# The opening of a two-block forward pass: sums on TensorE, modulation chunks on VectorE, loads behind the weight tiles

## The chip, the cores and the metric

The kernel runs on one core of a Trainium2 chip, in one launch. The metric is the device time in microseconds. Each instruction is issued on one of five engines, each in its own order: TensorE (PE; its weight loads are shown as PEld), VectorE (DVE), ScalarE (ACT), GpSimd (POOL) and SyncE (SP), from whose queue all the loads are issued.

## The reference

Two blocks work on 256 tokens of width 2048 in fp32. The opening computes the keys and values of the memory for a cross-attention, which are needed much later, and what the first product of the first block needs: the modulation and the root mean square of x.

```
mkv   = rms_norm(mem, g_mem) @ w_mem_kv          # 256 x 2048 @ 2048 x 1024
c_act = silu(c)
mod   = c_act @ w_ada + b_ada                    # 2048 x 6144
shift, scale, gate = split(mod, 3)
h     = rms(x, norm_g) * (1 + scale) + shift
proj  = h @ w_in                                 # 2048 x 8192: the next phase
```

Then come attention, a gated recurrence, the output product, and a second block with a latent attention, the cross-attention and a feed-forward part.

## The kernel before, in words

Weights come in tiles of 1 MB (four chunks of 128 rows, 512 columns) into three buffers `wr`. A product in nearly full precision is made of three: each weight tile is split into hi, a cast by ScalarE (`wh`), and lo, the remainder, a subtraction by VectorE (`wl`); the activations have hi and lo too. `split_w` does this for half a tile, two chunks; `job` then issues its matmuls. In the opening (phase `mem`) such a half is 12 matmuls with 512 columns. There are three buffers of `wh` and two of `wl`, so the lo piece of a half waits until TensorE is through with the half before last.

The opening multiplies eight tiles of `w_mem_kv`, four for K and four for V in turn, by the memory (`mH`, `mL`, made in `load_mem` by `gsplit`, lines 316 and 317). Beside it stands `front()`, a generator which `linear` advances after each tile. It does three things by the table `FRONT`. First it loads eight tiles of `w_ada`, scale and shift in turn (`ada_steps((4, 0), ...)`), and adds their chunks, each times its column of `cact`, into an accumulator: the scale's all on VectorE (`V`), of the shift's tile one on VectorE and three as a product on ScalarE and an addition on GpSimd (lines 387 to 391). `ada_sum` adds the accumulators over the partitions by matmuls against a matrix of ones, and VectorE takes one column of each. Second it loads x. Third it finds the token sums: `sumsq` squares on ScalarE and adds four tiles into one on GpSimd (line 250), for x and likewise for the memory; `token_R` sums over the partitions by 8 matmuls with 128 columns of ones, GpSimd makes the inverse root (`inv_rms`), VectorE scales an identity by it, and a matmul spreads it as `R2`. At the end `make_h(0)` scales x by `gs` and `R2` and adds the shift.

The order on each engine is set by a scheduler from the order in which the code issues the instructions and from their dependences. SP's queue keeps its order too: a load whose buffer is not free holds all behind it.

Of the kernel before, what the change touches and what calls it, by code (L numbers as in the profile page):

```python
# [13 lines left out]
AF = mybir.ActivationFunctionType  # L14
# [3 lines left out]
P = 128  # L18
T = 256
# [13 lines left out]
AHEAD = dict(mem=0, pass0=0, pass3=1, gz=0, az=1, out=0, in2=1, mla=1, o=0, ffn=1, down=0)  # L33
BUDGET = dict(mem=0.3, pass0=0.5, pass3=2.0, gz=1.3, az=1.1, out=0.5, in2=0.1, mla=0.9, o=0.6, ffn=0.1, down=0.3)


GATES = ("VVVV", "VVVV", "VVVV", "VVVV")
PAIR = ("VVVV", "VVVV")

EARLY = 3  # L40
GSTART = 10
FRONT = (2, 0, 1, 0, 1, 1, 3, 2)

LAG = 5
COST = (0.5, 0.4, 1.0, 0.7, 1.3)
# [15 lines left out]
def trunk_kernel(ctx, tc, a, out):  # L61
# [64 lines left out]
        S.copy(hi, src)  # L126
        V.tensor_tensor(lo, src, hi.bitcast(F32), ALU.subtract)

    jobs = deque()

    def submit(job):

# [8 lines left out]
    def tile_mm(src, kc0, kt, cw, mode, banks, act, first, last, pre=None, post=None, mid=None):  # L141

        raw = load(src, kt, cw)
        n = 2 if mode == "N" else cw // P
        nk = 4 if cw == 256 else 2

        def one(kc, b, hi, lo):
            xh, xl, xx = act(kc0 + kc)  # L150
            hi, lo = hi[:, kc % nk, :], lo[:, kc % nk, :]
            st, sp = first and kc == 0, last and kc == kt - 1
            if mode == "T":
                o = banks[b // 2][:, (b % 2) * T : (b % 2) * T + T]
                s = slice(b * P, b * P + P)
                trip = ((o, hi[:, s], xh), (o, hi[:, s], xl), (o, lo[:, s], xh))
                st = st and b % 2 == 0
            elif mode == "T2":
                s = slice(b * P, b * P + P)
                trip = ((two(banks[b]), hi[:, s], xx), (banks[b][:, :T], lo[:, s], xh))  # L160
            else:
                o = banks[b][:, :cw]
                s = slice(b * P, b * P + P)
                trip = ((o, xh[:, s], hi), (o, xh[:, s], lo), (o, xl[:, s], hi))
            for i, (d, l, r) in enumerate(trip):
                PE.matmul(d, l, r, start=st and i == 0, stop=sp and i == len(trip) - 1, skip_group_check=True)  # L166

        def job(k, hi, lo):
            if k == 0 and pre is not None:
                pre()  # L170
            if not banks:
                banks.extend(bank("mm") for _ in range((cw // P + 1) // 2 if mode == "T" else 2))
            pairs = [(kc, b) for kc in range(k, k + nk) for b in range(n)]
            if last and k + nk == kt:
                pairs.sort(key=lambda p: p[1])
            for kc, b in pairs:
                one(kc, b, hi, lo)
            drain(BUDGET[phase[0]])
            if k + nk == kt and post is not None:
                post()  # L180
            elif mid is not None:
                mid()

        for k in range(0, kt, nk):
            hi, lo = split_w(raw, k, cw, mode)
            submit(lambda k=k, hi=hi, lo=lo: job(k, hi, lo))
# [34 lines left out]
    def token_R(work, R, rc):  # L221


        ps = bank("ax")
        for tb in range(2):
            for k in range(4):
                PE.matmul(ps[:, tb * P : tb * P + P], work[:, k, tb * P : tb * P + P], ones, start=k == 0, stop=k == 3,  # L227
                          skip_group_check=True)
        for tb in range(2):
            V.tensor_copy(rc[:, tb : tb + 1], ps[:, tb * P : tb * P + 1])  # L230
        inv_rms(rc, rc, 1.0 / D, EPS)
        if R is None:
            return
        dg = tmp([P, 2, P], "R")
        for tb in range(2):
            V.tensor_scalar(dg[:, tb, :], ident, rc[:, tb : tb + 1], None, ALU.mult)

        def spread():
            ps = bank("ax")[:, :T]
            PE.matmul(ps, ones, flat(dg), start=True, stop=True)  # L240
            S.copy(R, ps)
        return spread
# [67 lines left out]
    cact = hpool.tile([P, DC], F32, tag="cact", name="cact")  # L310
    rm = hpool.tile([P, 2], F32, tag="rm", name="rm")
    ssm = hpool.tile([P, 4, 2], F32, tag="ssm", name="ssm")
    sums = slot("s7", [P, 8, T])

    def gsplit(j, gname, x, H, L):
        S.activation(H, x, AF.Identity, scale=col(gname, j))
# [26 lines left out]
    def load_mem(kg):  # L343
        c = slice(4 * kg, 4 * kg + 4)
        SP.dma_start(mem[:, c, :], a["memT"][:, c, :])
        for k in range(4 * kg, 4 * kg + 4):
            gsplit(k, "g_mem", mem[:, k, :], mH(k), mL(k))
        sumsq(mem[:, c, :], kg, sums[:, 0:4, :], work[:, 8:12, :])


    def load_x(j):
        c = slice(4 * j, 4 * j + 4)
        x = xt[j // 2][:, 4 * (j % 2) : 4 * (j % 2) + 4, :]
        SP.dma_start(x, a["xT"][:, c, :])
        sumsq(x, j, sums[:, 4:8, :], work[:, 12:16, :])

    n_ada = [0]

# [9 lines left out]
            return ada_raw[n_ada[0] % 2]  # L368
        return None

    def ada_tile(ng, kg, accs, plan):

        raw = ada_buf(ng)
        if raw is None:
            raw = load(a["w_ada"][ng, kg], 4, 512)
        else:
            SP.dma_start(raw, a["w_ada"][ng, kg].rearrange("p (k c) -> p k c", k=4))
        def chunk(k):
            cc = cact[:, 4 * kg + k : 4 * kg + k + 1]
            first = kg == 0 and plan[k] not in plan[:k]  # L380
            if plan[k] == "V":
                if first:
                    V.tensor_scalar(accs[0], raw[:, k, :], cc, None, ALU.mult)
                else:
                    V.scalar_tensor_tensor(accs[0], raw[:, k, :], cc, accs[0], ALU.mult, ALU.add)  # L385
            elif first:
                S.mul(accs[1], raw[:, k, :], cc)
            else:
                t = tmp([P, 512], "pts")
                S.mul(t, raw[:, k, :], cc)  # L390
                G.tensor_tensor(accs[1], accs[1], t, ALU.add)

        for k in range(4):
            chunk(k)
            if k == 1:
                yield

    def ada_sum(ng, accs):
        ps = bank("ax")
        for j in range(4):  # L400
            for i, acc in enumerate(accs):
                PE.matmul(ps[:, j * P : j * P + P], acc[:, j * P : j * P + P], ones, start=i == 0, stop=i == len(accs) - 1,  # L402
                          skip_group_check=True)
        V.tensor_tensor(modT[:, 4 * ng : 4 * ng + 4], ps.rearrange("p (j n) -> p j n", j=4)[:, :, 0],
                        colr("b_ada", 4 * ng, 4), ALU.add)

    def ada_steps(ngs, plans):

        accs = []
        for i, plan in enumerate(plans):  # L410
            if ngs[0] >= 8:
                one = tmp([P, 512], "acc", 1)
                accs.append((one, gate_acc2(ngs[0])) if len(set(plan)) == 2 else (one, one))
                continue
            work = slot("s8", [P, 2, 512]) if i else None
            accs.append((tmp([P, 512], "acc", 1) if i == 0 else work[:, 0], work[:, 1] if i else tmp([P, 512], "acc", 1))
                        if len(set(plan)) == 2 else (tmp([P, 512], "acc", 1) if i == 0 else slot("s8", [P, 512]),) * 2)
        for kg in range(4):
            for i, ng in enumerate(ngs):
                yield from ada_tile(ng, kg, accs[i], plans[i])  # L420
                if kg == 3 and i:
                    yield
                    yield
                if kg == 3:
                    f = lambda ng=ng, i=i: ada_sum(ng, accs[i][: len(set(plans[i]))])
                    if ng < 8:
                        f()
                    else:
                        later(0.1, lambda f=f, ng=ng: (f(), done.add(f"g{ng}")), evq)
# [17 lines left out]
    acth = lambda kc: pair_of(h1[0], kc)  # L447

    def front():
        steps = ada_steps((4, 0), ("VVVV", "VPPP"))  # L450
        for i, n in enumerate(FRONT):
            for _ in range(2 * n):
                next(steps, None)
            if 1 <= i <= 4:
                load_x(i - 1)
            if i == 5:
                spread = token_R(sums[:, 4:8, :], R2, r2)
            if i == 6:
                spread()
            if i == 7:  # L460
                make_h(0)
            yield
            yield

    S.activation(cact, colr("c"), AF.Silu)
    linear([(lambda kg: a["w_mem_kv"][0, kg], 512, "N", ev_memk),
            (lambda kg: a["w_mem_kv"][1, kg], 512, "N", ev_memv)], range(4), lambda kc: (mH(kc), mL(kc), None),
           ahead=load_mem, aside=front(), done_loads=lambda: token_R(sums[:, 0:4, :], None, rm))


    lbt = hpool.tile([P, 3, 8], F32, tag="lbt", name="lbt")
# [335 lines left out]
    def gate_steps():  # L807
        for ng in range(8, 12):
            while ng == 11 and not xp:
                yield  # L810
            yield from ada_steps((ng,), (GATES[ng - 8],))
            while f"g{ng}" not in done:
                yield

# [3 lines left out]
    def modulate(kg, n):  # L818

        if len(steps) == kg:  # L820
            steps.append(ada_steps((4 + kg + 1, kg + 1), PAIR) if kg < 3 else gates)
        if n % 4 < EARLY and (kg < 3 or n >= GSTART):
            next(steps[-1], None)

# [636 lines left out]
```

## Time and profile before

| what | us |
|---|---|
| median of 3 runs | 1591.23 |
| lowest and highest of them | 1588.77, 1593.85 |
| the profiled execution | 1593.98 |
| its span in the trace | 1592.20 |
| busy in the span: TensorE | 1534.7 |
| busy: VectorE, ScalarE, GpSimd | 1165.7, 823.0, 280.5 |

A row of a timeline gives the start in the span, the time that the merged instructions took, engine, line, operation, the tile written and those read, and in brackets how long the engine had stood idle and what it had waited for. The matmuls of one row overlap, so a row lasts longer than the distance to the next one. In a row by stretch, PEclk is the mean granted clock: 1.00 is 2.4 GHz and 0.50 is 1.2.

### The profile page before, as it was taken

To read this page: it belongs to the slowest core of one execution; us is meant where nothing else is said; L and a number is where in the kernel's file an instruction comes from. 1 tells how busy PE (TensorE), PEld (TensorE's weight loads), DVE (VectorE), ACT (ScalarE), POOL (GpSimd) and SP (SyncE) were. 2 spreads that over 40 slices of the span, in tenths; PEclk is the share of its full clock that TensorE was granted. 3 is DMA by queue.
4 is the path that set the end of the run, shared out by engine and by line. 5 is a ranking of instruction groups with operands and counts; after the bars stand their busy time and mean duration, and the time that the engine had idled before them with its cause. 6 is when DMAs were issued, how large, how long until landed. Compare 5 with 4: busy or idle time off the path is not lost.

```text
span 1592.2 us, 24722 instructions
## 1 busy us (share of the span) xinstructions
PE 1534.7 (96%) x9730; PEld 1384.7 (87%) x9730; DVE 1165.7 (73%) x1671; ACT 823.0 (52%) x1194; POOL 280.5 (18%) x309
## 2 busy tenths in 40 slices
PE   5799999999899999999999999999999999999998
PEld 4588988978889999987999888888888888888887
DVE  7788999899997778568667667667667667445444
ACT  6365443664546745468545555555555555333332
POOL 3500000156532011413001111111111111000000
PEclk9899999999999999999999999999999999999999
DMA  9478888444555476444435555555555555556553
GB/s 386 197 271 334 330 303 330 169 152 169 222 197 211 174 266 236 174 160 143 150 134 184 185 192 205 186 190 203 189 189 204 190 188 200 196 186 214 207 185 133
DMA packets 50803, 331.67 MB, mean 208 GB/s; under 512 B 5632, under 2 KB 7936, under 8 KB 13312
## 3 DMA queue, kind: packets, MB, share of 16 engines
q1 hardware_dynamic: 50688, 330.10, 57.4%
q8 instruction: 76, 1.25, 0.3%
q14 instruction: 39, 0.32, 0.1%
HBM read 327.98 MB, written 2.10 MB: 207 GB/s over the span
## 4 chain that ended last, share of the span: by engine, by line
PE 85%; DVE 9%; issue 2%; POOL 2%; ACT 2%; DMA 1%; SPq 0%; DVEq 0%; ACTq 0%; POOLq 0%
PE mm L166 80%; DVE wl L122 3%; DVE acc L385 2%; DMA wr<-in_w_mem_kv_dram 1%; ACT wh L121 1%; PE ax L731 1%; DVE y L732 1%; PE ax L227 1%; PE ax L529 1%; PE ax L402 1%; DVE R L704 0%; DVE y L712 0%; PE ax L521 0%; PE ax L257 0%; DVE s L317 0%
## 5 line engine op out<-in xcount | busy, mean ns | idle before, releaser
L122 DVE TENSOR_TENSOR wl<-wr,wh 128x1024 fp32r<-128x1024 f32 (+2 forms) x516 | 652.5, 1266 | 321.9 <-PE mm L166 298.9
L121 ACT CAST wh<-wr 128x1024 fp32r<-128x1024 f32 (+2 forms) x516 | 534.6, 1040 | 495.4 <-PE mm L166 421.1
L166 PE MATMUL mm<-h,wh 128*128 128x512 f32 (+1 forms) x2560 | 687.3, 342 | 0.9 <-ACT wh L121 0.9
L166 PE MATMUL mm<-h,wl 128*128 128x256 f32 x1984 | 551.4, 278 | 10.9 <-DVE wl L122 10.9
L166 PEld LDWEIGHTS mm<-h,wh 128*128 128x128 f32 x2560 | 441.8, 189 | 56.6 <-ACT wh L121 1.5
L166 PEld LDWEIGHTS mm<-h,wl 128*128 128x128 f32 x1984 | 373.4, 188 | 13.5 <-DVE wl L122 13.4
L166 PE MATMUL mm<-f,wh 128*128 128x512 f32 x704 | 239.4, 389 | 0.0
L166 PE MATMUL mm<-wh,h 128*128 128x512 f32 (+1 forms) x704 | 218.8, 386 | 0.0
L166 PE MATMUL mm<-f,wl 128*128 128x256 f32 x704 | 194.3, 276 | 0.0
L166 PE MATMUL mm<-y,wh 128*128 128x256 f32 x1024 | 182.5, 282 | 0.6 <-ACT wh L121 0.6
L166 PEld LDWEIGHTS mm<-y,wh 128*128 128x128 f32 x1024 | 155.6, 189 | 0.9 <-ACT wh L121 0.8
L166 PEld LDWEIGHTS mm<-f,wh 128*128 128x128 f32 x704 | 132.2, 188 | 27.7
L166 PEld LDWEIGHTS mm<-wh,h 128*128 128x128 f32 x704 | 131.4, 188 | 24.5
L166 PE MATMUL mm<-y,wl 128*128 128x256 f32 x512 | 142.9, 280 | 2.6 <-DVE wl L122 2.5
L166 PE MATMUL mm<-wl,h 128*128 128x512 f32 (+1 forms) x352 | 135.6, 385 | 2.4 <-DVE wl L122 2.3
L166 PEld LDWEIGHTS mm<-f,wl 128*128 128x128 f32 x704 | 132.2, 188 | 0.0
L166 PEld LDWEIGHTS mm<-y,wl 128*128 128x128 f32 x512 | 96.5, 189 | 3.5 <-DVE wl L122 3.4
L1299 POOL TENSOR_TENSOR gp<-sg,R 128x256 f32<-128x256 f32 x44 | 36.1, 822 | 314.2 <-DVE sg L1298 314.2
L166 PEld LDWEIGHTS mm<-wl,h 128*128 128x128 f32 x352 | 66.3, 188 | 15.9 <-DVE wl L122 4.3
L166 PE MATMUL mm<-wh,s 128*128 128x512 f32 x128 | 45.3, 434 | 9.8 <-ACT wh L121 9.8
L385 DVE SCALAR_TENSOR_TENSOR acc<-wr,cact,acc 128x512 f32<-128x512 f32 x60 | 49.9, 831 | 0.3
L641 DVE TENSOR_TENSOR s<-mm,s 128x512 f32<-128x512 f32 x72 | 49.0, 682 | 0.9 <-PE mm L166 0.7
(299 smaller groups left out, 1477.8 us busy)
## 6 DMA issues: line engine op xcount, KB each, us to landing
wr<-in_w_in_dram SPq DMA_DIRECT2D x76, 1024.0 KB, 4.9
wr<-in_w_gate_dram SPq DMA_DIRECT2D x44, 1024.0 KB, 4.9
wr<-in_w_up_dram SPq DMA_DIRECT2D x44, 1024.0 KB, 4.8
wr<-in_w_down_dram SPq DMA_DIRECT2D x40, 1024.0 KB, 4.9
y<-in_w_ada_dram SPq DMA_DIRECT2D x28, 1024.0 KB, 7.2
wr<-in_w_ada_dram SPq DMA_DIRECT2D x16, 1024.0 KB, 5.1
wr<-in_w_out_dram SPq DMA_DIRECT2D x16, 1024.0 KB, 4.8
wr<-in_w_o_dram SPq DMA_DIRECT2D x16, 1024.0 KB, 4.8
```

What stands on the lines that cost most here:

```text
L121: S.copy(hi, raw[:, k : k + n, :])
L122: V.tensor_tensor(lo, raw[:, k : k + n, :], hi.bitcast(F32), ALU.subtract)
L166: PE.matmul(d, l, r, start=st and i == 0, stop=sp and i == len(trip) - 1, skip_group_check=True)
L227: PE.matmul(ps[:, tb * P : tb * P + P], work[:, k, tb * P : tb * P + P], ones, start=k == 0, stop=k == 3, skip_group_check=True)
L385: V.scalar_tensor_tensor(accs[0], raw[:, k, :], cc, accs[0], ALU.mult, ALU.add)
L402: PE.matmul(ps[:, j * P : j * P + P], acc[:, j * P : j * P + P], ones, start=i == 0, stop=i == len(accs) - 1, skip_group_check=True)
L529: PE.matmul(po[:, :T], vblk(0), t[:, :T], start=True, stop=False, skip_group_check=True)
L641: V.tensor_tensor(d, b, d, ALU.add)
L731: PE.matmul(ps[:, j, b, :], k2[:, j, s], q2[:, j, s], start=True, stop=True)
L732: V.copy_predicated(AT[:, :, 0:2, :].rearrange("p h b t -> p h (b t)"), bc(hgm[:, li - 1, :], 2), ps.rearrange("p h b t -> p h (b t)"))
L1299: G.tensor_tensor(gp[:, 2:], s, R3, ALU.mult)
```

## The change

`front()` is no longer a generator beside the tiles. It fills a table `at`, from the number of a half to functions, and `job` calls those of its half after its matmuls. The loads of the `w_ada` tiles are issued one behind each tile of `w_mem_kv` (but for the last pair, which goes together), and the loads of x in two pairs. All eight tiles' chunks are on VectorE, mostly one of the scale and one of the shift behind a half. The squares stay on ScalarE, but are no longer added on GpSimd: for each of the eight squared tiles `token_sums` issues 8 matmuls with the square as the stationary operand and one column of ones, which accumulate in one bank, `tsum`. `ada_sum` too streams one column of ones. The options for chunks on ScalarE and GpSimd are gone; the other uses of `ada_steps` had all their chunks on VectorE already.

```
-GATES = ("VVVV", "VVVV", "VVVV", "VVVV")
-PAIR = ("VVVV", "VVVV")
-FRONT = (2, 0, 1, 0, 1, 1, 3, 2)
+    jobs, at, halves = deque(), {}, [0]
             drain(BUDGET[phase[0]])
+            for f in at.pop(halves[0], ()):
+                f()
+            halves[0] += 1
...
-        sumsq(mem[:, c, :], kg, sums[:, 0:4, :], work[:, 8:12, :])
+        S.activation(work[:, 8:12, :], mem[:, c, :], AF.Square)
+    tsum = []
+    def token_sums(src, j, o):
+        first = not tsum
+        if first:
+            tsum.append(bank("ax"))
+        for tb in range(2):
+            for k in range(4):
+                PE.matmul(tsum[0][:, o + tb : o + tb + 1], src[:, k, tb * P : tb * P + P], ones[:, 0:1],
+                          start=first and tb == k == 0, stop=j == 3 and k == 3, skip_group_check=True)
+    def token_rms(dst, o):
+        V.tensor_copy(dst, tsum[0][:, o : o + 2])
+        inv_rms(dst, dst, 1.0 / D, EPS)
...
-            for i, acc in enumerate(accs):
-                PE.matmul(ps[:, j * P : j * P + P], acc[:, j * P : j * P + P], ones, start=i == 0, stop=i == len(accs) - 1,
-                          skip_group_check=True)
+            PE.matmul(ps[:, j : j + 1], acc[:, j * P : j * P + P], ones[:, 0:1], start=j == 0, stop=True, skip_group_check=True)
...
+        for kg in range(4):
+            put(4 * kg, fetch, 4, kg)
+            put(4 * kg + (2 if kg < 3 else 0), fetch, 0, kg)
+            put(4 * kg + 1, token_sums, work[:, 8:12, :], kg, 0)
+        for j in range(4):
+            put(4 * (j // 2) + 2, load_x, j)
+        for h, kg, ks in ((2, 0, (0,)), (3, 0, (1,)), (4, 0, (2,)), (5, 0, (3,)), (6, 1, (0,)), (7, 1, (1,)), (8, 1, (2,)),
+                          (9, 1, (3,)), (10, 2, (0,)), (11, 2, (1,)), (12, 2, (2, 3)), (13, 3, range(4))):
+            put(h, chunks, kg, ks)
+        for h, j in ((3, 0), (4, 1), (7, 2), (8, 3)):
+            put(h, x_squares, j)
+            put(h + 1, token_sums, work[:, 12:16, :], j, 2)
+        put(10, lambda: spread.append(x_spread()))
+        put(11, lambda: spread[0]())
+        put(13, ada_sum, 4, scale)
+        put(13, ada_sum, 0, shift)
+        put(15, make_h, 0)
```

What the scheduler makes of it is seen in the order on each engine. First VectorE around the lo pieces of halves 9 to 12, where x's sums are turned into `R`; here before. `wl` is a lo piece, `acc` and `s_153` are the accumulators of scale and shift, `s_99` a lo part of the memory, `r_78` and `R` the token's inverse root and the scaled identity:

```order
L122 TENSOR_TENSOR wl<-wr,wh 128x1024 x2
L385 SCALAR_TENSOR_TENSOR s_153<-memwork,cact,s_153 128x512
L122 TENSOR_TENSOR wl<-wr,wh 128x1024 x2
L385 SCALAR_TENSOR_TENSOR acc<-s_390,cact,acc 128x512
L230 COPY r_78<-ax 128x1 x2
L385 SCALAR_TENSOR_TENSOR acc<-s_390,cact,acc 128x512
L236 TENSOR_SCALAR R<-ident,r_78 128x128
```

The lo pieces of halves 9 to 12 stand ahead of the copy of the sums, and chunks between the steps to `R`. And now (`s_106` is the shift's accumulator):

```order
L407 SCALAR_TENSOR_TENSOR s_106<-memwork,cact,s_106 128x512 x4
L317 SCALAR_TENSOR_TENSOR s_99<-memwork,cols,s_97 128x256 x4
L363 COPY r_78<-ax 128x2
L237 TENSOR_SCALAR R<-ident,r_78 128x128 x2
L117 TENSOR_TENSOR wl<-wr,wh 128x1024 x2
L407 SCALAR_TENSOR_TENSOR acc<-s_352,cact,acc 128x512 x4
L117 TENSOR_TENSOR wl<-wr,wh 128x1024 x2
```

The copy and both scalings have moved ahead of the lo pieces of halves 9 and 10, and chunks stand four together. Now TensorE at the same place; before, the sums stand ahead of half 11 (`s_103` is the sum of squares, `s_97` and `s_99` the memory's hi and lo):

```order
L166 MATMUL mm<-wl,s_97 128x512
L166 MATMUL mm<-wh,s_99 128x512
L227 MATMUL ax<-ones,s_103 128x128 x8
L166 MATMUL mm<-wh,s_97 128x512 x2
L166 MATMUL mm<-wl,s_97 128x512
```

And now, ahead of half 9 (`memwork` holds the squares); three such groups of 8 calls stand ahead of half 5 too, one ahead of half 1 and one ahead of half 13:

```order
L162 MATMUL mm<-wl,s_96 128x512
L162 MATMUL mm<-wh,s_98 128x512
L359 MATMUL ax<-ones,memwork 128x1 x24
L162 MATMUL mm<-wh,s_97 128x512 x2
L241 MATMUL ax<-R,ones 128x256
L162 MATMUL mm<-wl,s_97 128x512
```

24 calls stand where 8 stood, two halves earlier, and the spread of `R` stands between a half's hi and lo matmuls.

## Rows read from the trace of the kernel before

**Rows 1.** Busy time by stretch: engines, granted clock, DMA share.
```profile
145.00:213.00 68.00, 68.00 (x402) 60.47 (x401) 63.53 (x86) 30.10 (x34) 0.00 (x0) 1.00 0.89 334
```

**Rows 2.** Waits of 0:90: total us, times, longest us.
```profile
PE mm L166 <- DVE wl L122: 16.4, 5, 8.7
...
PE mm L166 <- ACT wh L121: 9.9, 2, 9.8
```

**Rows 3.** Timeline of TensorE, matmuls and weight loads: start, us, instructions, idle before.
```profile
9.76 1.22 PE L166 MATMUL mm<-wh,s 128*128 128x512 f32 x2 [9.76 <-ACT wh L121]
...
20.41 0.62 PE L166 MATMUL mm<-wh,s 128*128 128x512 f32 x2
...
21.09 0.62 PE L166 MATMUL mm<-wh,s 128*128 128x512 f32 x2
...
36.94 0.79 PE L166 MATMUL mm<-wl,s 128*128 128x512 f32 x1 [5.92 <-DVE wl L122]
...
38.38 1.05 PE L166 MATMUL mm<-wh,s 128*128 128x512 f32 x2
...
39.66 1.05 PE L166 MATMUL mm<-wh,s 128*128 128x512 f32 x2
...
51.96 3.68 PE L227 MATMUL ax<-ones,s 128*128 128x128 f32 x16 [1.97 <-POOL s L250]
...
51.96 3.39 PEld L227 LDWEIGHTS ax<-ones,s 128*128 128x128 f32 x16 [2.39 <-POOL s L250]
...
70.31 0.80 PE L166 MATMUL mm<-wl,s 128*128 128x512 f32 x1 [8.73 <-DVE wl L122]
...
79.45 1.86 PEld L227 LDWEIGHTS ax<-ones,s 128*128 128x128 f32 x16 [0.28 <-issue]
...
82.60 0.70 PE L166 MATMUL mm<-wh,s 128*128 128x512 f32 x2
...
89.86 0.74 PE L166 MATMUL mm<-h,wh 128*128 128x256 f32 x4 [0.19 <-ACT wh L121]
```

**Rows 4.** Timeline of VectorE.
```profile
19.92 1.66 DVE L317 SCALAR_TENSOR_TENSOR s<-memwork,cols,s 128x256 fp32r<-128x256 f32 x4
...
26.26 7.34 DVE L385 SCALAR_TENSOR_TENSOR acc<-y,cact,acc 128x512 f32<-128x512 f32 x4
...
57.45 2.43 DVE L236 TENSOR_SCALAR R<-ident,r 128x128 f32<-128x128 f32 x1 [0.89 <-POOL r L214]
...
62.36 5.69 DVE L317 SCALAR_TENSOR_TENSOR s<-memwork,cols,s 128x256 fp32r<-128x256 f32 x4
...
71.97 3.10 DVE L385 SCALAR_TENSOR_TENSOR acc<-y,cact,acc 128x512 f32<-128x512 f32 x4
...
82.08 1.22 DVE L122 TENSOR_TENSOR wl<-wr,wh 128x1024 fp32r<-128x1024 f32 x1
```

**Rows 5.** Timeline of GpSimd.
```profile
60.20 8.97 POOL L391 TENSOR_TENSOR s<-s,pts 128x512 f32<-128x512 f32 x6 [0.40 <-ACT pts L390]
```

**Rows 6.** Timeline of ScalarE.
```profile
7.73 1.04 ACT L247 ACTIVATE s<-memwork 128x1024 f32<-128x1024 f32 x1
```

**Rows 7.** Busy time by microsecond, with the granted clock (PEclk).
```profile
41.00:42.00 1.00, 1.00 (x4) 0.81 (x3) 0.76 (x1) 0.39 (x1) 0.00 (x0) 0.57 1.06 422
...
52.00:53.00 1.00, 1.00 (x5) 1.00 (x6) 1.00 (x2) 0.00 (x0) 0.00 (x0) 0.55 1.00 418
...
55.00:56.00 1.00, 1.00 (x7) 0.92 (x6) 0.32 (x3) 0.00 (x0) 0.01 (x1) 0.74 0.97 410
...
66.00:67.00 1.00, 0.00 (x0) 0.00 (x0) 1.00 (x2) 0.60 (x1) 0.92 (x2) 0.50 0.00 0
...
76.00:77.00 1.00, 1.00 (x6) 0.81 (x5) 0.00 (x0) 0.00 (x0) 0.00 (x0) 1.00 0.50 66
```

**Rows 8.** Timeline of SP's queue.
```profile
45.76 0.33 SPq L109 DMA_DIRECT2D wr<-in_w_mem_kv_dram  x1
...
75.82 0.33 SPq L377 DMA_DIRECT2D y<-in_w_ada_dram  x1
```

More of the change, by code (lines that the diff above doesn't have):

```diff
@@ L127, in split @@
         V.tensor_tensor(lo, src, hi.bitcast(F32), ALU.subtract)
-    jobs = deque()
+    jobs, at, halves = deque(), {}, [0]
     def submit(job):
@@ L231, in token_R, with spread_R @@
         inv_rms(rc, rc, 1.0 / D, EPS)
-        if R is None:
-            return
+        return spread_R(R, rc)
+    def spread_R(R, rc):
         dg = tmp([P, 2, P], "R")
@@ L312, in trunk_kernel @@
     ssm = hpool.tile([P, 4, 2], F32, tag="ssm", name="ssm")
-    sums = slot("s7", [P, 8, T])
     def gsplit(j, gname, x, H, L):
@@ L347, in load_mem, with x_part, x_squares, x_spread @@
             gsplit(k, "g_mem", mem[:, k, :], mH(k), mL(k))
-        sumsq(mem[:, c, :], kg, sums[:, 0:4, :], work[:, 8:12, :])
-    def load_x(j):
[L352 to L355, printed above, removed]
+        S.activation(work[:, 8:12, :], mem[:, c, :], AF.Square)
[11 more added lines that the diff above has]
+        inv_rms(dst, dst, 1.0 / D, EPS)
+    def x_part(j):
+        return xt[j // 2][:, 4 * (j % 2) : 4 * (j % 2) + 4, :]
+    def load_x(j):
+        SP.dma_start(x_part(j), a["xT"][:, 4 * j : 4 * j + 4, :])
+    def x_squares(j):
+        S.activation(work[:, 12:16, :], x_part(j), AF.Square)
+    def x_spread():
+        token_rms(r2, 2)
+        return spread_R(R2, r2)
     n_ada = [0]
@@ L369, in ada_buf, with ada_load @@
         return None
-    def ada_tile(ng, kg, accs, plan):
+    def ada_load(ng, kg):
         raw = ada_buf(ng)
         if raw is None:
-            raw = load(a["w_ada"][ng, kg], 4, 512)
-        else:
[L377 to L391, printed above, removed]
+            return load(a["w_ada"][ng, kg], 4, 512)
+        SP.dma_start(raw, a["w_ada"][ng, kg].rearrange("p (k c) -> p k c", k=4))
+        return raw
@@ L393, in ada_tile, with ada_chunk, ada_sum @@
+    def ada_chunk(raw, k, kg, acc):
+        cc = cact[:, 4 * kg + k : 4 * kg + k + 1]
+        if kg == k == 0:
+            V.tensor_scalar(acc, raw[:, k, :], cc, None, ALU.mult)
+        else:
+            V.scalar_tensor_tensor(acc, raw[:, k, :], cc, acc, ALU.mult, ALU.add)
+    def ada_tile(ng, kg, acc):
+        raw = ada_load(ng, kg)
         for k in range(4):
-            chunk(k)
+            ada_chunk(raw, k, kg, acc)
             if k == 1:
                 yield
-    def ada_sum(ng, accs):
+    def ada_sum(ng, acc):
@@ L399, in ada_sum @@
         ps = bank("ax")
         for j in range(4):
-            for i, acc in enumerate(accs):
-                PE.matmul(ps[:, j * P : j * P + P], acc[:, j * P : j * P + P], ones, start=i == 0, stop=i == len(accs) - 1,
-                          skip_group_check=True)
[L404 to L417, printed above, removed]
+            PE.matmul(ps[:, j : j + 1], acc[:, j * P : j * P + P], ones[:, 0:1], start=j == 0, stop=True, skip_group_check=True)
@@ L418, in ada_steps @@
+        V.tensor_tensor(modT[:, 4 * ng : 4 * ng + 4], ps[:, 0:4], colr("b_ada", 4 * ng, 4), ALU.add)
+    def ada_steps(ngs):
+        accs = [slot("s8", [P, 512]) if i else tmp([P, 512], "acc", 1) for i in range(len(ngs))]
         for kg in range(4):
             for i, ng in enumerate(ngs):
-                yield from ada_tile(ng, kg, accs[i], plans[i])
+                yield from ada_tile(ng, kg, accs[i])
                 if kg == 3 and i:
@@ L424, in ada_steps @@
                 if kg == 3:
-                    f = lambda ng=ng, i=i: ada_sum(ng, accs[i][: len(set(plans[i]))])
+                    f = lambda ng=ng, i=i: ada_sum(ng, accs[i])
                     if ng < 8:
@@ L449, in front, with chunks, put, fetch @@
     def front():
[L450 to L463, printed above, removed]
+        scale, shift = tmp([P, 512], "acc", 1), slot("s8", [P, 512])
+        raws, spread = {}, []
+        def chunks(kg, ks):
+            for k in ks:
+                ada_chunk(raws[4, kg], k, kg, scale)
+                ada_chunk(raws[0, kg], k, kg, shift)
+        def put(h, f, *args):
+            at.setdefault(h, []).append(lambda: f(*args))
+        def fetch(ng, kg):
+            raws[ng, kg] = ada_load(ng, kg)
+        for kg in range(4):
[15 more added lines that the diff above has]
+        put(15, make_h, 0)
     S.activation(cact, colr("c"), AF.Silu)
+    front()
     linear([(lambda kg: a["w_mem_kv"][0, kg], 512, "N", ev_memk),
             (lambda kg: a["w_mem_kv"][1, kg], 512, "N", ev_memv)], range(4), lambda kc: (mH(kc), mL(kc), None),
-           ahead=load_mem, aside=front(), done_loads=lambda: token_R(sums[:, 0:4, :], None, rm))
+           ahead=load_mem, done_loads=lambda: token_rms(rm, 0))
     lbt = hpool.tile([P, 3, 8], F32, tag="lbt", name="lbt")
@@ L810, in gate_steps @@
                 yield
-            yield from ada_steps((ng,), (GATES[ng - 8],))
+            yield from ada_steps((ng,))
             while f"g{ng}" not in done:
@@ L820, in modulate @@
         if len(steps) == kg:
-            steps.append(ada_steps((4 + kg + 1, kg + 1), PAIR) if kg < 3 else gates)
+            steps.append(ada_steps((4 + kg + 1, kg + 1)) if kg < 3 else gates)
         if n % 4 < EARLY and (kg < 3 or n >= GSTART):
```

## The prediction

> **What bounds the kernel now.** The stages are read first: from 145 to 213 us TensorE is busy 68.00 of 68 us [rows 1], so what the opening gives back moves everything behind it forward and is not swallowed there. The opening is where TensorE stands. By the waits of its first 90 us it waits 16.4 us for VectorE's lo pieces (`wl`), in five stops of which the longest is 8.7, and 9.9 for ScalarE's first cast [rows 2]. The timeline of TensorE places them [rows 3]: first matmul at 9.76, stops of 5.92 before 36.94, 1.97 before 51.96 (for GpSimd) and 8.73 before 70.31; the memory product ends at 89.86 less 0.19 = 89.67 us. That is the mark: call each stretch of 12 matmuls on one pair of hi and lo pieces a half, 16 in all, and ask when half 16 ends.
>
> Why is VectorE late? Its own rows tell [rows 4, 5]. Four chunks of modulation take 3.10 us at 71.97, when GpSimd is idle, and 7.34 at 26.26; four lo parts of the memory take 1.66 at 19.92 and 5.69 at 62.36, inside the 8.97 us in which GpSimd adds products of chunks. So beside an adding GpSimd VectorE's work takes two to three times as long: 4.2 and 4.0 us lost at these two places alone, and behind them TensorE's two longest stops.
>
> **What the change takes away and what it adds.** Quiet durations: a lo piece 1.22 us, four chunks 3.1, four lo parts 1.66 [rows 4]; 12 matmuls at the full clock 12 x 0.227 = 2.72, from three in 0.68 us between 20.41 and 21.09; at the lower level 0.427 each, from three in 1.28 between 38.38 and 39.66 [rows 3].
>
> Away: all GpSimd adds of the opening, and with them the slowing of VectorE; also ScalarE's 12 products of shift chunks. Added: those 12 chunks go to VectorE, 12 x 0.75 = 9 us, paid out of the time it no longer loses. On TensorE the two token sums of 8 calls become 64 calls with one column. In the trace a call in full fp32 is two instructions (16 rows for 8 calls), so 128 instructions stand for 32; the opening's two modulation sums go from 24 instructions to 16, and those of the ten later sums, 8 each, stay as many. The price of such an instruction is the largest unknown: the trace has none with one column. With 128 columns the weight loads follow each other at 1.86/16 = 0.116 us at the full clock and 3.39/16 = 0.212 at the lower level [rows 3]. One column still needs its 128x128 weights loaded; a stream of one column instead of 128 can only make it shorter. Above, the bound is 0.212, if the clock is down; below, it is nothing. I take 0.116, the row nearest in kind, since the load is the same.
>
> Here the Trainium skill has two rules (TensorE: Matmul & The Clock Gate). Its section Back-to-back issue gap gives matmuls of 1 to 64 columns about 25 ns each, by which the 144 instructions would take 3.6 us. Its section LDWEIGHTS says that loading takes the stationary columns divided by 1.2 in ns, whatever streams behind, 107 ns for 128 columns, which gives 15.4 us and speaks against moving sums to TensorE this way.
>
> The walk, with the order of the changed kernel:
> (a) ScalarE's square of the first memory tile ends at 7.73 + 1.04 = 8.77 [rows 6]. TensorE's 16 sum instructions now stand ahead of the first matmul, at the lower level: 16 x 0.212 = 3.4, to 12.2. After a start the lower level lasted from 36.94 to about 41.8, and from 70.31 to 76.0 [rows 3, 7]; with 5.7 us of it, 5 matmuls are slow (2.1) and 19 fast (4.3): halves 1 and 2 end at 18.6, halves 3 and 4 at 24.1.
> (b) 48 sum instructions: 5.6, to 29.7. Halves 5 to 8: 10.9, to 40.6. The 5.92 us stop goes: the lo pieces of halves 5 and 6 are made under the sums, and four chunks behind them are quiet.
> (c) 48 again: to 46.2. Now a new wait. VectorE's copy of the sums and two scalings of R stand ahead of the lo pieces of halves 9 and 10, so TensorE waits for a chain: from the sums' end (51.96 + 3.68 = 55.64) to the first scaling (57.45) it took 1.8 us [rows 3, 4], two scalings about 0.2 each (an estimate, from a quiet 128x256 part at 1.66/4 = 0.42), a lo piece 1.22: to 49.6. Behind these wait the rest of VectorE's queue and TensorE itself. After a stop of 1.97 us the clock was down from about 52.1 to 55.5 [rows 7]; this one is about 2.9, so I add half of 3.4 = 1.7. 22 more matmuls (two run before the wait): 5.0. Halves 9 and 10 end at 56.3, 11 and 12 at 61.8.
> (d) 16 sum instructions, a copy and a lo piece on VectorE (1.9 + 0.2 + 1.2): to 65.1; halves 13 and 14 end at 70.1.
> (e) Then the modulation. VectorE makes two lo pieces from 63.9, eight chunks (6.2) and two sums' small operations, to 72.9; TensorE's shift sum (8 instructions, 0.9) follows, then three scalings of x (1.3) and the lo piece of half 15: 76.3. 22 matmuls 5.0, and 1.7 again for a clock that fell while TensorE did 16 short instructions: half 16 ends at 83.0. The before does the same with two long stops: halves 13 and 14 start at 70.31, half 15 at 82.60.
>
> So 89.67 - 83.0 = 6.7 us sooner. About 0.5 of it I give back for semaphores that the walk leaves out: 6.2 us. Nothing is charged for DMA: the last weight tile was issued at 45.76 [rows 8], as its buffer came free; here that is after the lo pieces of half 10, at about 52, 24 us before its use. SP's first modulation load of the next phase waits, now as before, for the last chunks of this one (75.82 in before, about 73 here), and the second projection tile waits behind it on SP; it is needed after the first one's work, so some 10 us remain. ScalarE's casts of the last tile now stand behind its copies and squares of K; they are costed at nothing because VectorE is busy with chunks and x until 75. If either cover went, TensorE would wait by what the piece is late.
>
> The profiled execution took 1593.98 us, span 1592.20 and 1.78 around it; 1593.98 - 6.2 = 1587.8. That execution is 2.75 above the median of 1591.23, so against the median: 1585.0 us. About 0.3%, 4.8 us, is what a measurement can tell from no change.
>
> **The rivals.**
> A, slower: the one-column sums run at the lower level. Nothing streams through TensorE but one column per load, and in the trace the clock went down while TensorE stood [rows 7]. If it goes down in every such stretch, all 144 instructions cost 0.212: those of (a) already do, the other 128 add 128 x 0.096 = 12.3, and half 5 starts slow as half 9 does (1.7): half 16 ends at 97.5, 7.8 later, 1599. It decides from 0.16 us an instruction, where the sum turns to nothing. For it: the price and the clock of such work are not in the trace. Against: the trace's 128-column sums at 79.45 kept 0.116.
> A', the clock goes down part of the way through the two long stretches: about 24 instructions of each slow (2 x 2.3), half 5 slow (1.7): half 16 at 89.8, no change, 1591.
> B, the sums are cheap: at 0.05 (about midway between nothing and 0.116) the walk loses 112 x 0.066 = 7.4 us and VectorE, with its 16 lo pieces, 32 chunks and parts, takes over a part: half 16 at about 77, 1579. This is the side of the skill's first rule.
> C, VectorE was not slowed by GpSimd but by something that stays: then the stops remain and the gain is gone (1591), and if half of the 9 us of added chunks comes on top, 1596. Against: it is quick at each place where GpSimd idles.
>
> **Chances.** The walk's case, 1580 to 1590, 0.50; B 0.15; A' 0.18; A 0.10; C 0.07. Faster by over 0.3% (below 1586.4): 0.41 of the walk's, 0.15 of B, 0.02 of A': 0.58. Within: 0.09, 0.16 of A', 0.02 of A and 0.03 of C: 0.30. Slower: 0.08 and 0.04: 0.12. The range goes 2 us beyond B's time and on the other side into A, whose instructions may lie anywhere between the two prices: 1577 to 1596; beyond it I leave some 0.07 at either end.
>
> **What would show it.** In the profile after: GpSimd with nothing but small operations in the opening; `acc` and `s` chunks all near 0.75 us and lo pieces at 1.22; no stop of 5 us or more; a stop near 46 to 50 us that ends with a lo piece behind R. One-column instructions at 0.11 us each with the granted clock at 1.00 bear out the price; at 0.2 with 0.50 they make A. The first `mm<-h,wh` about 6 us sooner than 89.86, and that distance kept at the end. Wrong it would be if the distance shrank behind the opening, or if TensorE waited there for a projection tile.

## The result and the profile after

The changed kernel takes 1603.11 us (median of 6 runs, 1599.92 to 1607.29) where the kernel before takes 1591.41 (6 runs): a ratio of 1.0074, 95% interval 1.0062 to 1.0087. The forecast was 1585.0, the range 1577 to 1596: wrong in sign. The profiled execution of after, 1599.92, is its fastest, and that of before lies above its median; so these two traces lie 5.9 us apart in their spans, the medians 11.7. One execution of an experiment below (e8_128_and_stand) ran with the clock near 0.55 from end to end; it is left out of its numbers, and its rows come from a second run.

The mark first. Half 16 ends when the first matmul on `h` starts: 100.55 us, against 89.86 before [rows 3], so the opening is 10.7 us longer and not 6.2 shorter. The timeline of TensorE after (start, us, instructions, what it reads, idle time before):

```profile
24.58 1.84 PE L359 MATMUL ax<-ones,memwork 128*128 128x1 f32 x16
30.15 6.99 PE L359 MATMUL ax<-ones,memwork 128*128 128x1 f32 x32 [3.74 <-ACT memwork L348]
37.00 1.20 PE L162 MATMUL mm<-wh,s 128*128 128x512 f32 x2
...
50.83 1.84 PE L359 MATMUL ax<-ones,memwork 128*128 128x1 f32 x16
56.41 6.99 PE L359 MATMUL ax<-ones,memwork 128*128 128x1 f32 x32 [3.74 <-ACT memwork L348]
63.25 1.20 PE L162 MATMUL mm<-wh,s 128*128 128x512 f32 x2
...
78.79 1.84 PE L359 MATMUL ax<-ones,memwork 128*128 128x1 f32 x16
80.49 0.72 PE L162 MATMUL mm<-wh,s 128*128 128x512 f32 x2
...
100.55 0.40 PE L162 MATMUL mm<-h,wh 128*128 128x256 f32 x2
```

Each group of 48 sum instructions (the rows on `memwork`, 16 and then 32) takes 12.4 us: 24.58 to 37.00 and 50.83 to 63.25. Between the 16 and the 32 TensorE stands 3.74 us for ScalarE's square of the memory, and the 32 take 6.84 us (30.15 to 37.00: 0.214 each), the 16 ahead of half 13 only 1.70 (78.79 to 80.49: 0.106 each). ScalarE's timeline at the first stand:

```profile
17.57 1.05 ACT L374 ACTIVATE memwork<-y 128x1024 f32<-128x1024 f32 x1
26.50 1.06 ACT L374 ACTIVATE memwork<-y 128x1024 f32<-128x1024 f32 x1 [7.88 <-PE ax L359]
27.46 1.69 ACT L316 ACTIVATE s<-memwork,cols 128x256 fp32r<-128x256 f32 x4
29.06 1.04 ACT L348 ACTIVATE memwork<-memwork 128x1024 f32<-128x1024 f32 x1
30.00 2.92 ACT L116 CAST wh<-wr 128x1024 fp32r<-128x1024 f32 x3
```

The square of x part 0 has been ready since 18.6. That of part 1 goes into the same buffer, so it waits 7.88 us until TensorE has summed part 0, which its order does only behind half 4. Behind it stand four hi pieces of the memory and the square that TensorE then wants. The stretches of a microsecond or two (busy time of PE, PEld, DVE, ACT, POOL, then the granted clock, DMA share and GB/s) show the clock:

```profile
0.00:97.00 97.00, 76.49 (x324) 64.68 (x325) 53.08 (x86) 39.84 (x69) 5.86 (x12) 0.81 0.64 255
28.00:29.00 1.00, 0.00 (x0) 0.00 (x0) 1.00 (x3) 1.00 (x3) 0.00 (x0) 1.00 0.93 381
29.00:30.00 1.00, 0.00 (x0) 0.00 (x0) 0.67 (x2) 1.00 (x2) 0.00 (x0) 0.70 1.04 418
30.00:31.00 1.00, 0.85 (x4) 0.85 (x5) 0.00 (x0) 1.00 (x3) 0.00 (x0) 0.50 1.02 410
42.00:43.00 1.00, 1.00 (x4) 0.81 (x3) 0.87 (x1) 0.50 (x1) 0.00 (x0) 0.50 0.98 397
43.00:44.00 1.00, 1.00 (x5) 0.77 (x5) 0.36 (x1) 1.00 (x2) 0.00 (x0) 0.97 0.54 213
```

It falls to 1.2 GHz (0.50) at about 29.4, in the stand, and stays there to 43.1: through 6.8 us of sums without a gap, then through 6 us of halves 5 and 6. In the second group it falls at 53.3, 0.7 us into the stand, and is back at 70.4. At the start of a trace this column can't be taken at its word: it reads 1.00 from 0 us on, while the 16 sums at 8.29 take 0.212 us each and the first 512-column matmuls 0.427, the pace of the lower level [rows 3].

The first row shows what came as forecast: GpSimd has 5.86 us of work left in the opening. VectorE's four chunks take 3.11 us everywhere (7.34 beside GpSimd's additions before [rows 4]), and TensorE's waits for lo pieces, 16.4 us before [rows 2], are gone but for two of 0.82 and 1.35:

```profile
27.99 1.68 DVE L317 SCALAR_TENSOR_TENSOR s<-memwork,cols,s 128x256 fp32r<-128x256 f32 x4 [4.83 <-ACT s L316]
...
33.35 3.11 DVE L407 SCALAR_TENSOR_TENSOR acc<-y,cact,acc 128x512 f32<-128x512 f32 x4
```

Its own 4.83 us of idling ahead of the lo parts comes from the same hi pieces.

### The profile page after: what moved, and what is told of

It is laid out like the page before. It is cut to its first block, busy times and chain, and to the rows that moved or that the text cites. A ratio compares the mean times of both kernels' runs of the same rounds, so it can differ in the third digit from the quotient of the medians.

```text
span 1598.1 us, 24854 instructions
## 1 busy us (share of the span) xinstructions
PE 1550.6 (97%) x9818; PEld 1401.7 (88%) x9818; DVE 1151.8 (72%) x1681; ACT 816.5 (51%) x1182; POOL 248.7 (16%) x292
## 4 chain that ended last, share of the span: by engine, by line
PE 85%; DVE 9%; issue 2%; DMA 2%; ACT 1%; POOL 1%; SPq 0%; DVEq 0%; ACTq 0%; POOLq 0%
PE mm L162 80%; DVE wl L117 3%; DVE acc L407 2%; DMA wr<-in_w_mem_kv_dram 1%; PE ax L359 1%; DVE y L758 1%; PE ax L419 1%; PE ax L555 1%; PE ax L757 1%; DVE y L738 0%; PE ax L258 0%; DVE R L730 0%; PE ax L547 0%; PE ax L683 0%; PE ax L1241 0%
## 5 line engine op out<-in xcount | busy, mean ns | idle before, releaser
L117 DVE TENSOR_TENSOR wl<-wr,wh 128x1024 fp32r<-128x1024 f32 (+2 forms) x516 | 641.6, 1245 | 331.9 <-PE mm L162 307.9
L162 PEld LDWEIGHTS mm<-wh,h 128*128 128x128 f32 x704 | 131.4, 188 | 24.6
```

Source lines behind the costliest of these rows:

```text
L117: V.tensor_tensor(lo, raw[:, k : k + n, :], hi.bitcast(F32), ALU.subtract)
```

## The experiments

Half 16 is the start of the first matmul on `h` in the profile; the ratio is that to the runs of before on the same chip.

| kernel | median us | ratio, 95% interval | half 16 |
|---|---|---|---|
| before | 1591.41 | | 89.86 |
| after | 1603.11 | 1.0074, 1.0062 to 1.0087 | 100.55 |
| e1_two_buffers | 1589.55 | 0.9987, 0.9977 to 0.9997 | 91.56 |
| e2_gpsimd_adds | 1590.71 | 1.0001, 0.9993 to 1.0010 | 87.10 |
| e4_spread | 1584.58 | 0.9970, 0.9959 to 0.9981 | 84.44 |
| e5_128_columns | 1578.23 | 0.9928, 0.9916 to 0.9940 | 79.03 |
| e6_128_together | 1577.99 | 0.9916, 0.9896 to 0.9937 | 78.59 |
| e8_128_and_stand | 1582.30 | 0.9942, 0.9921 to 0.9963 | 78.63 |
| e7_spread_128 | 1576.52 | 0.9913, 0.9893 to 0.9932 | 72.86 |
| e9_one_pass | 1574.01 | 0.9898, 0.9881 to 0.9915 | 72.88 |
| e10_sums_apart | 1572.59 | 0.9886, 0.9866 to 0.9906 | 69.61 |

**e1_two_buffers: the wait alone is taken away.**

```diff
+    sq2 = slot("s7", [P, 8, T])
+    def mem_sq(kg):
+        return work[:, 8:12, :] if kg % 2 == 0 else sq2[:, 4:8, :]
+    def x_sq(j):
+        return work[:, 12:16, :] if j % 2 == 0 else sq2[:, 0:4, :]
...
-        S.activation(work[:, 12:16, :], x_part(j), AF.Square)
+        S.activation(x_sq(j), x_part(j), AF.Square)
```

> The changed kernel with a second buffer for the squares of x and one for those of the memory (their order and number stay). Theory 1 (ScalarE's square of x part 1 waits until TensorE has summed part 0, and behind it stand the hi pieces; TensorE then stands 3.74 us twice and its clock falls): both stands go, the sums run at 0.107 us instead of 0.214, half 16 ends near 80 instead of 100.55, and the time is 1580 to 1586 us. Theory 2 (the long rows of one-column sums bring the clock down by themselves): only the stands go, 32 sums still take 6.8 us, half 16 ends near 93 and the time is 1594 to 1598. Theory 3 (the loads and chunks as they are now set bound the opening): half 16 stays past 97, the time at 1600 or more.

Measured: both stands are gone, and the time is that of before. But the clock falls all the same. The first group of sums and the clock around it:

```profile
26.07 1.84 PE L366 MATMUL ax<-ones,memwork 128*128 128x1 f32 x16
27.77 6.50 PE L366 MATMUL ax<-ones,s 128*128 128x1 f32 x32
34.13 1.20 PE L162 MATMUL mm<-wh,s 128*128 128x512 f32 x2
```

```profile
26.00:28.00 2.00, 2.00 (x21) 1.96 (x19) 2.00 (x3) 0.34 (x1) 0.00 (x0) 1.00 1.00 414
28.00:29.00 1.00, 1.00 (x8) 1.00 (x8) 1.00 (x2) 0.70 (x1) 0.00 (x0) 0.65 1.01 418
30.00:32.00 2.00, 2.00 (x11) 2.00 (x11) 1.50 (x2) 0.00 (x0) 0.00 (x0) 0.50 1.02 397
...
38.00:39.00 1.00, 1.00 (x5) 0.73 (x4) 0.00 (x0) 0.00 (x0) 0.00 (x0) 0.73 1.03 426
```

TensorE is busy 1.00 in every row, and at about 28.3 us (0.65 is three tenths of that microsecond at 1.00), 2.2 us into one-column sums, the clock drops to 0.50; the 32 sums take 6.36 us, and it is back only at 38.5, behind 4.4 us of 512-column matmuls. In the second group it falls at 52.2, 5.0 us into 48 such sums. Theory 1 explains the stands and not this; theory 2 said 93 for half 16 and comes nearest with 91.56, though its time, 1594 to 1598, is over 4 us longer than the median. (The profiled execution, 1595.62, is the longest of the twelve; its clock is down once more for 10 us from 451.5, far behind the opening.)

**e2_gpsimd_adds: the sums go back.** `sumsq` with its additions on GpSimd and `token_R` as before; loads and chunks stay as the change has them.

```diff
-        S.activation(work[:, 12:16, :], x_part(j), AF.Square)
+        sumsq(x_part(j), j, sums[:, 4:8, :], work[:, 12:16, :])
...
-        token_rms(r2, 2)
-        return spread_R(R2, r2)
+        return token_R(sums[:, 4:8, :], R2, r2)
```

> The changed kernel with the squares added on GpSimd again and summed by 128-column matmuls at the end, as before; loads and chunks stay as the change has them. Theory 1 and theory 2: no stand at 26 and 52 us and no one-column sums, so half 16 ends between 80 and 88 and the time is 1580 to 1592 us. Theory 3: half 16 stays past 97 and the time at 1600 or more.

Measured: 87.10 and no change against before, so theory 3 falls, as in e1_two_buffers: the 12 us come with the new sums. It also shows that loads and chunks alone bring nothing, since VectorE is slow again wherever GpSimd adds. VectorE and GpSimd around 40 us:

```profile
30.87 3.11 DVE L394 SCALAR_TENSOR_TENSOR acc<-y,cact,acc 128x512 f32<-128x512 f32 x4
...
39.46 7.11 DVE L394 SCALAR_TENSOR_TENSOR s<-memwork,cact,s 128x512 f32<-128x512 f32 x4
```

```profile
39.63 5.60 POOL L253 TENSOR_TENSOR s<-s,memwork 128x1024 f32<-128x1024 f32 x2 [1.17 <-ACT memwork L252]
```

Four chunks take 3.11 us, and 7.11 beside 5.60 us of additions.

**e5_128_columns: only the columns are changed,** `ones` for `ones[:, 0:1]`, each sum with 128 columns of the bank.

> The changed kernel with the 128 sum instructions streaming 128 columns of ones instead of one; the single buffers and the stands stay. If one-column work is what keeps the clock down once the stand has brought it down (theory 2 in part), the clock rises within the 32 sums after the stand, they take less than 6 us instead of 6.84, and half 16 ends 4 to 10 us sooner than at 100.55. If the stand alone sets the clock (theory 1), the sums take 32 x 0.23 = 7.4 us at the lower level, and half 16 ends at 100 to 102, 1600 to 1606 us.

25 us off, far more than either theory said. But the scheduler, which goes by the instructions' sizes, had also moved ScalarE's square of x part 1 behind the hi pieces and the square of the memory, so that TensorE no longer stands there, and had split the groups of calls: this run doesn't tell columns from order. In the next two the order of the sums and squares is held in the code (`tc.issue_after`, which queues an instruction behind another on its engine).

**e6_128_together: e1_two_buffers with 128 columns, its order held** as far as the end of half 8.

```diff
+                with tc.issue_after(mm_last[0].ins):
+                    token_sums(*args)
...
-                PE.matmul(tsum[0][:, o + tb : o + tb + 1], src[:, k, tb * P : tb * P + P], ones[:, 0:1],
+                PE.matmul(tsum[0][:, (o + tb) * P : (o + tb + 1) * P], src[:, k, tb * P : tb * P + P], ones,
```

> Two buffers and the order of e1_two_buffers (24 sum calls together ahead of halves 5 and 9), but each sum instruction streams 128 columns of ones instead of one. If one-column work brought the clock down in that run (it fell at 28.6 us, with TensorE busy without a gap), the clock stays at 1.00 here, the 48 instructions take 48 x 0.116 = 5.6 us instead of 8.1, the half behind them 2.8 instead of 4.4, and half 16 ends 6 to 12 us sooner than at 91.6: 1577 to 1583 us. If it was something else at that place (loads, the shorter wait for VectorE), the clock falls here too, at 28 to 30 us, and the time is 1588 to 1594.

```profile
24.50 1.95 PE L382 MATMUL ax<-ones,memwork 128*128 128x128 f32 x16
26.29 3.74 PE L382 MATMUL ax<-ones,s 128*128 128x128 f32 x32
```

```profile
28.00:29.00 1.00, 1.00 (x12) 1.00 (x11) 0.96 (x2) 0.92 (x1) 0.00 (x0) 1.00 0.96 385
30.00:32.00 2.00, 2.00 (x11) 1.64 (x10) 0.00 (x0) 0.00 (x0) 0.00 (x0) 1.00 0.98 395
```

The same 48 instructions at the same place: 5.3 us (24.50 to the first matmul at 29.78) instead of 8.1, the clock 1.00 throughout. Up to the end of half 8 the order on TensorE and ScalarE is that of e1, and there e6 is 6.4 us ahead (40.76 against 47.19). So the one-column stream brought the clock down. The mean granted clock of each whole execution agrees, though it holds the stages behind the opening too: 0.983 to 0.986 in the six of after, 0.986 to 0.992 in the twelve of e1, 0.994 to 0.997 in the four of e6.

Half 16 ends 13 us sooner than in e1, the time is 11.6 less, but not all of that is the columns'. Behind half 8 the orders part: in e1 the matmul that spreads R and its wait stand ahead of half 9 (in after inside it); in e6 the lo pieces of halves 9 and 10 come first and the spread of R stands behind half 12, without a wait. Here e1, then e6:

```profile
54.70 1.22 PE L241 MATMUL ax<-R,ones 128*128 128x256 f32 x2 [1.84 <-DVE R L237]
```

```profile
57.01 0.59 PE L241 MATMUL ax<-R,ones 128*128 128x256 f32 x2
```

**e8_128_and_stand: the single buffers of after with 128 columns,** the order of after held up to half 9 (the second group and the spread of R stand otherwise than in after).

> The single buffers of the changed kernel, its order up to half 9 (24 sum calls ahead of half 5, ScalarE's square of x part 1 ahead of the hi pieces of the memory), with 128 columns in each sum instruction. The stand of 3.7 us ahead of half 5 is there again by both theories. If the stand by itself also brings the clock down, the 32 sums behind it start at the lower level, but the clock is back sooner than behind one-column sums, which took 6.84 us at 0.50 and 6 us of matmuls more. If only the one-column sums do it, the clock stays at 1.00 from 20 to 45 us. Half 16 ends between 82 and 95, the time is 1582 to 1595 us.

Its three other runs gave 1579.97, 1582.30 and 1583.67 us, their median at the near end of the range; half 16, at 78.63, came sooner than the 82 to 95 expected. For the rows it was run once more, 1580.42 us:

> e8_128_and_stand once more, for a profile at the full clock (its first was taken while the clock was near 0.55 over the whole program). TensorE stands 3.7 us ahead of half 5 behind the first 16 sums. If a stand of that length by itself brings the clock down, 1 us or more of the stretch 24 to 45 us shows 0.50 with 128-column sums too; if not, the clock stays at 1.00 there and the 32 sums behind the stand take 3.7 us instead of 6.84.

```profile
23.61 1.95 PE L375 MATMUL ax<-ones,memwork 128*128 128x128 f32 x16
29.29 5.47 PE L375 MATMUL ax<-ones,memwork 128*128 128x128 f32 x32 [3.74 <-ACT memwork L360]
34.51 0.48 PE L162 MATMUL mm<-wh,s 128*128 128x512 f32 x1
```

```profile
29.00:30.00 1.00, 0.71 (x6) 0.71 (x7) 0.96 (x2) 1.00 (x2) 0.00 (x0) 1.00 0.98 397
30.00:31.00 1.00, 1.00 (x9) 1.00 (x9) 1.00 (x2) 1.00 (x2) 0.00 (x0) 0.82 1.02 410
...
33.00:34.00 1.00, 1.00 (x6) 1.00 (x6) 0.96 (x3) 0.00 (x0) 0.00 (x0) 0.50 1.01 410
34.00:35.00 1.00, 1.00 (x8) 0.96 (x8) 0.96 (x3) 0.16 (x1) 0.00 (x0) 0.98 0.99 406
```

The stand of 3.74 us is there, and it too brings the clock down, but only at 30.6, 1.3 us after work had begun again. Here 128-column sums bring it back at 34.0; in after one-column sums left it at 0.50 until 43. So both causes hold. By the medians 128 columns bring 20.8 us with the stand (1603.11 to 1582.30) and 11.6 without (1589.55 to 1577.99); in both pairs the spread of R moved too, so a part of both is the order's. The second buffer brings 13.6 with one column. With 128 its 4.3 us can't be told from nothing: the intervals of e6 and e8 overlap, and half 16 ends at 78.59 and 78.63.

**e4_spread and e7_spread_128: the sums apart.** Two buffers, each set of 8 calls behind a half of its own, and the spread of R one half later, in e4 with one column, in e7 with 128.

```diff
-            put(h + 1, token_sums, work[:, 12:16, :], j, 2)
+            put((4, 6, 8, 10)[j], behind, token_sums, x_sq(j), j, 2)
...
+        def behind(f, *args):
+            with tc.issue_after(mm_last[0].ins):
+                f(*args)
```

> Two buffers for each kind of square, and each set of 8 sum calls put behind a half of its own, so that no more than 16 one-column instructions follow each other. Theory 1: little beside two buffers alone, half 16 within 3 us of it, 76 to 80, and 1576 to 1584 us. Theory 2: the clock stays up only here, half 16 ends near 78 here against 93 with the sums still together. Theory 3: past 97 in both.

> The spread sums of e4_spread (one set of 8 calls behind a half of its own, two buffers), with 128 columns. There the clock was 1.00 up to 40 us with 16 one-column instructions at a time, so little is to be gained by the columns: half 16 ends within 3 us of 84.4, 1579 to 1586 us. If one-column sums of this length cost clock too (the 0.83 of 40 to 50 us), 4 to 7 us sooner, 1576 to 1580.

In e4 the clock stays at 1.00 through the first four sets, 16 one-column instructions each. It falls at 44.1, behind a stand of 1.74 us for a cast and in one of 0.53:

```profile
43.20 0.73 PE L162 MATMUL mm<-wh,s 128*128 128x512 f32 x2 [1.74 <-ACT wh L116]
44.46 0.79 PE L162 MATMUL mm<-wl,s 128*128 128x512 f32 x1 [0.53 <-DVE wl L117]
```

It falls again at 74.9, behind the modulation's one-column sums; half 16 at 84.44 misses the theories. In e7 there is no stand above 0.2 us from 10 us on and no fall up to 73 (its PEclk is 1.00 in every ten): 72.86, sooner than both of its expectations. ScalarE's order differs by one square: in e4 the square that waits for TensorE (5.28 us, to 38.61) stands ahead of the memory's hi pieces and square, in e7 behind them, so the casts start at 42.12 in e4 and at 39.58 in e7. So what lies between e4 and e7 is columns and stands together.

**e9_one_pass and e10_sums_apart: how far does it go?** In e9 the squares and the ones are fp32r, so a call is one instruction; in e10 the modulation's sums stream 128 columns too, and the shift's stand behind half 15.

```diff
+    sq2 = slot("s7", [P, 8, T], F32R)
+    onesr = tmps[0].tile([P, P], F32R, tag="pts", name="onesr")
+    V.tensor_copy(onesr, ones)
...
-        put(13, ada_sum, 0, shift)
+        put(14, behind, ada_sum, 0, shift)
```

> The spread sums with 128 columns of e7_spread_128, but the squares are rounded to fp32r as ScalarE writes them and the ones are fp32r too, so that a sum call is one instruction instead of two: 64 instead of 128. (One buffer for each kind of square again; ScalarE's squares are put so late that the sums ahead of them are done.) In e7 TensorE is busy without a gap from 10 to 72 us, so if TensorE bounds the opening there, 64 x 0.112 = 7.2 us go and half 16 ends near 66 instead of 72.9, 1568 to 1572 us. If the loads or VectorE are next behind it, the stands grow in place of the sums, and the time is 1573 to 1577 us.

> e9_one_pass with the last one-column sums of the opening gone: the modulation's sums stream 128 columns, and those of the shift stand behind half 15 instead of six matmuls into it. In e9 the clock fell at 63.9 us, behind 8 one-pass and 8 one-column sums and a stand of 0.5 us, and came back at 71; six of the matmuls then waited for the sums of the shift. If the one-column sums had a part in that fall, the clock stays at 1.00, half 16 ends near 69 instead of 72.9, and the time is 1568 to 1573 us. If the short stand alone did it, or the modulated x is now late (TensorE stands ahead of the first matmul on h), half 16 ends at 71 or later or the gain is given back, and the time is 1573 to 1577 us.

e9 ends half 16 at 72.88, as e7 does: 7 us fewer of sums and nothing gained in the opening (the medians' 2.5 us are not told apart by the intervals). Its trace is that of the longest of four executions. What is next is seen at its end:

```profile
60.72 1.00 PE L368 MATMUL ax<-onesr,s 128*128 128x128 f32 x8
61.56 1.00 PE L428 MATMUL ax<-ones,acc 128*128 128x1 f32 x8
...
63.41 0.50 PE L162 MATMUL mm<-wl,s 128*128 128x512 f32 x1 [0.51 <-DVE wl L117]
...
65.40 1.70 PE L428 MATMUL ax<-ones,s 128*128 128x1 f32 x8
```

Eight one-column sums and a stand of 0.51, and the clock is at 0.50 from 63.8 to 70.6. With 128 columns there, e10 has the same stand (0.54) and keeps 1.00:

```profile
61.43 1.11 PE L428 MATMUL ax<-ones,acc 128*128 128x128 f32 x8
...
63.31 0.50 PE L162 MATMUL mm<-wl,s 128*128 128x512 f32 x1 [0.54 <-DVE wl L117]
...
65.98 1.05 PE L428 MATMUL ax<-ones,s 128*128 128x128 f32 x8
...
69.61 0.62 PE L162 MATMUL mm<-h,wh 128*128 128x256 f32 x2
```

```profile
64.00:66.00 2.00, 2.00 (x11) 1.60 (x10) 1.93 (x7) 0.44 (x1) 0.89 (x2) 1.00 0.97 410
66.00:68.00 2.00, 2.00 (x14) 1.82 (x13) 2.00 (x5) 2.00 (x11) 0.00 (x0) 1.00 1.01 426
```

Half 16 and the time are those of the first branch of its expectation. The fall in e9 came ahead of the shift's sums, so it wasn't their new place that kept the clock up in e10. That the columns did rests on one trace of each and isn't shown beyond them: the intervals of e9 and e10 overlap, and the mean granted clocks of their executions are 0.995 to 0.998 and 0.994 to 0.998. e10 is 17.4 us below the before of its runs (1590.03) and 30.5 below the changed kernel.

## Why the prediction was wrong

Its walk against the trace, in us:

| step | forecast | measured |
|---|---|---|
| (a) start to the end of half 4 | 24.1 | 24.6 |
| (b) 48 sum instructions | 5.6 | 12.4 |
| halves 5 to 8 | 10.9 | 13.8 |
| (c) 48 sum instructions | 5.6 | 12.4 |
| wait for R, halves 9 to 12 | 15.6 | 15.5 |
| (d) 16 sums, halves 13 and 14 | 8.3 | 8.4 |
| (e) modulation, halves 15 and 16 | 12.9 | 13.4 |

The steps sum to 83.0 and 100.5. What failed is (b), "48 sum instructions: 5.6, to 29.7", and the same in (c): 13.6 of the 17.5 us, and 2.9 more in the slow half behind (b). Both were counted as so many instructions at one price. Two things were left out.

First, who delivers the squares. The walk followed TensorE and VectorE, not ScalarE, and took the squares as ready. The diff shows one buffer for x's, and the order has all the sums of x parts 0 and 1 behind half 4: a wait of ScalarE for TensorE and of TensorE for ScalarE in one group. That is 3.74 us of each 6.8. The wait that (c) did foresee, for R, came as forecast (63.25 to the lo piece at 66.37). That halves 9 to 12 came out right behind it is in part luck: the walk charged 1.7 us for a clock that falls in the stop for R, and the trace paid for one that had been down since 53.3.

Second, the clock. The price was right: 0.106 to 0.107 us at the full clock, below the 0.116 taken, and with 128 columns it is the same 0.106 (16 in 1.70 in e7). So it isn't the streamed columns that set it, and rival B fell with that. The weight load, which both share, fits: by the Trainium skill (TensorE: Matmul & The Clock Gate, LDWEIGHTS) loading 128 columns takes 107 ns, and the trace agrees with 0.106. The 25 ns of that page's section Back-to-back issue gap no run here shows; the section gives them for matmuls by themselves and says that in a stream of weight loads and matmuls both set the spacing.

But of the 96 instructions in (b) and (c) 64 ran at 0.214, each group's 32 behind the stand: 3.4 us of each group. Rival A' is nearest to this, at 0.18: it had the clock go down part of the way through both groups, about 24 instructions of each, and half 5 slow, 1591 us. It did not have the stands; e1_two_buffers, without them, took 1589.55. Rival A, at 0.10, had all 144 at the lower level and 1599 us, 4 short of the median. A's "against", that 128-column sums kept 0.116, was about another stream: e1 beside e6 shows that a row at one column can't be read off one at 128, though each instruction costs the same.

What held: no chunk or lo piece slowed by GpSimd, the stops for lo pieces gone (rival C fell), (d) and (e), and no charge for DMA. What the prediction named as a sign of being wrong is in these two traces: the distance shrinks behind the opening, from 10.7 us at the first matmul on `h` to 5.9 at the end. Of this 2.9 came back by 123 us, on a stretch where before stood 0.70 and 1.11 us for lo pieces and after did not; the rest wasn't followed, and the medians lie 11.7 apart.

e6 and e7, without that stand and that fall, take 13 and 15 us off the before, more than the 6.2 that the walk gave it: there the matmul that spreads R stands behind half 12 (57.01 in e6) or half 13, and (c)'s wait for it is gone.

## What to carry to other kernels

When work moves to an engine, walk the engine that feeds it too: a buffer used twice, with its reader late in another engine's order, is a new wait, and a second buffer or an earlier reader takes it away. Ask what the moved work does to the clock of what comes behind it: 48 instructions in a row that stream one column cost as much each as with 128 and gave the clock away, where 16 in a row behind 512-column matmuls kept it (after, 78.79; e4_spread). And hold the order when one thing is to be changed, since e5_128_columns moved two at once, and compare the orders as far as the reading goes: e6_128_together was like e1_two_buffers only up to half 8.

## What the runs showed of the hardware that was not expected

- TensorE counted as busy 1.00 and still lost its clock: in e1_two_buffers at 28.3 us, 2.2 us into one-column sums, and again at 52.2, 5.0 us into them; with 128 columns at the same place it stayed at 1.00 (e6_128_together).
- Once down, the clock stayed at 0.50 through 6.84 us of one-column sums without a gap (after, 30.15 to 37.00) and 6 us of matmuls; through 128-column sums it was back 4.7 us after they began (e8_again, 29.29 to 34.0).
- Behind a stand of 3.74 us the clock was still 1.00 for 1.3 us of work and only then fell (e8_again, 30.6); in after, behind the same stand, it fell 0.7 us before work began, and in its second stand 3.1 us before.
- A sum in fp32 with 128x128 weights is two instructions a call, at the full clock 0.106 us each with one streamed column (16 in 1.70, after) and with 128 (16 in 1.70, e7_spread_128; 32 in 3.49, e6_128_together); in fp32r it is one, of 0.105 (8 in 0.84, e9_one_pass).
